# The first group's gather: token rows in two rounded parts, and one-pass products, in a hybrid decoder trunk

## The chip, the cores and the metric

The kernel runs on one core of a Trainium2 chip. The metric is the device time of one execution in microseconds. TensorE (PE) multiplies, VectorE (DVE), ScalarE (ACT) and GpSimd (POOL) do the elementwise work, and SyncE (SP) issues the large loads. 4-byte numbers come in two types here: fp32, whose product PE does in several passes, and fp32r, a rounded form whose product takes one pass.

## What is computed

Two layers work on 528 tokens of 1024 numbers: 16 meta tokens and 512 of the input. Layer 0 is a short convolution with gates, layer 1 is latent attention; each is followed by a mixture of experts. Of 64 experts of 256 columns, in 8 groups, each token picks one group, and in it the two best experts:

```
g_logits = xf @ w_grp ;  grp = argmax(g_logits)          # 8 groups
e_logits = xf @ w_exp                                    # 8 per group
top_p, top_i = top_k(softmax(e_logits of that group), 2)
gate   = p_g * top_p / sum(top_p)
expert = grp * 8 + top_i
out    = sum over both: gate * (silu(xn @ w_gate[e]) * (xn @ w_up[e])) @ w_down[e]
h      = h + out
```

## The kernel before

**Tiles.** The tokens lie in h as four tiles of 128 rows (0 to 3) and one of 16 (META, the tile hm). Layer 0 works on all five, layer 1 on the four.

**Weights.** A mixture of experts reads 192 MB per layer. `Ring` loads them in pieces of 1 MB over SP's queue into slots: four called A, up to 13 called R, and B, five in layer 0 and eight in layer 1. A slot takes the next piece of a fixed list as soon as its last reader is through. The B slots are opened at the start of `run`, in the order `LEFT[layer]`, in memory that the stage before used. SP's queue works in order: a load whose slot is not free holds up those behind it.

**The experts** run in 16 quads of four. gate_up (L589, gu) is the first product of each.

**The stretch around the change.** `project_out` (L266 to L298) does the last projection of a layer by three fp32r products of each pair of parts (L292) and adds it to h (L294). As soon as a tile of h is whole, `route` follows. It squares the rows (L231, ACT), transposes (L372), copies (L375 on ACT, L377 on DVE), multiplies for the logits (L380) and does the choice as a chain of small DVE instructions: gm, oh, mg, oh, se (L395), s (L397), eq, gt, eq, gt (L398 to L401), r and M (L402, L403). M says which experts a token has. `rank` (L411 to L425) counts tokens by a product with a triangle (L417) and makes from it rm (L418), d (L419) and aux (L421). d is the 0/1 matrix that picks the tokens of the first group.

`first_gather` (L457 to L477) collects the group's tokens. Each tile gives a small product pa (L467) and two products of 512 columns, d times h, in fp32 (L431, `gather_tile`), all accumulated in three banks. Behind the last tile come ag (L473, DVE), xg (L436, two instructions of ACT), sel (L441), the select (L450) and xT (L451), and then gate_up of quad 0. The later groups go through the same `gather_tile` from `run`. What stands where in an engine's row is decided by a scheduler from the order of the code and the data; `rank` of the last tile is put behind the third last tile's gather by hand.

Of the kernel before, what the change touches and what calls it, by code (L numbers as in the profile page):

```python
# [9 lines left out]
F32 = mybir.dt.float32  # L10
F32R = mybir.dt.float32r
BF16 = mybir.dt.bfloat16
I32 = mybir.dt.int32
AF = mybir.ActivationFunctionType
ALU = mybir.AluOpType
AX = mybir.AxisListType.X
ET = mybir.EngineType
PSUM = bass.MemoryType.PSUM

P = 128  # L20
D = 1024
# [9 lines left out]
SLOT = 2048  # L31
# [5 lines left out]
STEPS = ((0,), (1,), (2,), (3,), (4,), (5,), (6, 7)), ((4,), (5,), (6, 7))  # L37
NX = 3, 0
TOP = 13, 3
LEFT = range(5), (0, 1, 2, 4, 3, 5, 6, 7)  # L40
LAST = (0, 512), (512, D)
LATE = 12, 13

# [15 lines left out]
def rows(t):  # L59
    return NM if t == META else P  # L60
# [56 lines left out]
def trunk_kernel(ctx: ExitStack, tc: tile.TileContext, x, meta, const, masks, rope, gcol, grow, wr, w_in, w_out, w_a, w_qr, w_hp,  # L117
                 w_o, w_gate, w_up, w_down, out):
    nc = tc.nc
    V, A, T, G = nc.vector, nc.scalar, nc.tensor, nc.gpsimd  # L120
# [7 lines left out]
    h = [cp.tile([P, D], F32, name=f"h{t}") for t in range(4)] + [hm.tile([P, D], F32, name="hm")]  # L128
# [6 lines left out]
    for l in range(2):  # L135
        for a in range(4):
            c = G_FFN + 8 * l + 2 * a
# [114 lines left out]
    def pool(stack, name, bufs=1, side=None, space=None):  # L252
        kw = {} if space is None else {"space": space}
        return stack.enter_context(tc.tile_pool(name=name, bufs=bufs, side=side, reuse_waits="tile", **kw))
# [44 lines left out]
    class Moe:  # L299
# [124 lines left out]
                if s not in self.done:  # L424
                    T.matmul(self.rkv[:, s], one_b[:n], M[:n, t], start=False, stop=False, skip_group_check=True)  # L425

        def gather_tile(self, ps, t, first, last):

            n, d = rows(t), self.d[:rows(t), t].bitcast(F32)
            for u in range(2):  # L430
                i = T.matmul(ps[u], d, h[t][:n, 512 * u:512 * u + 512], start=first, stop=last, skip_group_check=True)  # L431
            return i

        def scaled_tokens(self, ps, ag):
            for u in range(2):
                A.activation(self.xg[:, :, 64 * u:64 * u + 64], ps[u].rearrange("s (p k) -> s k p", k=8), AF.Copy, scale=ag[:, 9:10])  # L436
# [17 lines left out]
        def new_ag(self):  # L454
            return self.ep.tile([P, 18], F32, tag="ag", name="ag", bufs=2)

        def first_gather(self, psum):  # L457

            def bank():
                return psum.tile([P, 512], F32, tag="acc", name="acc", bufs=5)  # L460

            self.sel = {}
            ps, pa = [bank(), bank()], bank()
            for t in self.done:
                first, last = t == self.done[0], t == self.done[-1]
                n = rows(t)
                T.matmul(pa[:, :10], self.d[:n, t].bitcast(F32), self.aux[:n, t, :10], start=first, stop=last)  # L467
                i = self.gather_tile(ps, t, first, last)
                if t == self.done[-3]:
                    with tc.issue_after(i.ins):  # L470
                        self.rank(self.done[-1])
            self.ag0 = self.new_ag()
            V.tensor_copy(self.ag0[:, :10], pa[:, :10])  # L473
            self.scaled_tokens(ps, self.ag0)
            self.choose(0, self.ag0)
            self.select(0, self.x0, bank)
# [63 lines left out]
        def run(self, limit, late, order, done=None, after=None, redo=None, again=None):  # L540

            layer, nT, tiles = self.layer, self.nT, self.tiles
            with ExitStack() as st:
                B = [(pool(st, f"ringB{layer}{i}"), f"B{i}") for i in range(NB[layer])]
                ring.open([B[i] for i in LEFT[layer]], limit)
                for a in ("gup", "psm", "ygp") if layer == 0 else ("psm", "gup", "ygp"):
# [323 lines left out]


    moe0 = Moe(0)
    with ExitStack() as l0:
        zp = pool(l0, "zp")
        zH = zp.tile([P, 8, NTOK], F32R, name="zH")
# [8 lines left out]
        with ExitStack() as l0a:  # L884
            wp = pool(l0a, "wp0", 2)
            psum = pool(l0a, "ps0", space=PSUM)
# [9 lines left out]
            def in_weights(j, s):  # L896
                raw = ring.get(("in", j, s))
                H, L = (wp.tile([P, SLOT], F32R, tag=a, name=a, bufs=2).rearrange("p (a c) -> p a c", a=8)
                        for a in ("wH", "wL"))
                for k in range(8):  # L900
                    i, _ = split_scaled(H[:, k], L[:, k], raw[:, k], gc[:, G_MIX0 + k:G_MIX0 + k + 1])
                ring.release(("in", j, s))
                loaded[j, s] = H, L
                return i
# [15 lines left out]
            first = in_weights(0, 0)  # L920
# [8 lines left out]
            for j in range(4):  # L929
                W = []  # L930
                for s in range(3):
# [3 lines left out]
                    for m in range(2):  # L935
                        mc = 2 * j + m
                        ps = psum.tile([P, 2, 512], F32, tag="acc", name="acc", bufs=3)
                        for k in range(8):
                            for l, r in ((wH, xH), (wH, xL), (wL, xH)):
                                for u in range(2):  # L940
                                    T.matmul(ps[:, u, :HALF], l[:, k, P * m:P * m + P], r[:, k, HALF * u:HALF * u + HALF],  # L941
                                             start=k == 0 and l is wH and r is xH, stop=k == 7 and l is wL)
                        pv = ps[:, :, :HALF]
                        if s == 0:
                            c = tp.tile([P, 2, HALF], F32, tag="c", name="c", bufs=2)
# [17 lines left out]
                            G.tensor_copy(zM[:, mc, :NM], acc[:, :NM])  # L963
        moe0.prepare(first_late)
        wp = pool(l0, "wp0b", 2)
        psum = pool(l0, "ps0b", space=PSUM)
        project_out(lambda j: [wp.tile([P, 512], F32R, tag=a, name=a) for a in ("wH", "wL")], psum, "out", zH, zL, zM, STEPS[0],
                    lambda t: moe0.route(t, psum))
        moe0.first_gather(psum)


    l1 = ExitStack()
# [27 lines left out]
    moe1 = Moe(1)  # L1000
# [4 lines left out]
    def weights(n):  # L1005
        return [wp.tile([P, SLOT], F32R, tag=a, name=a, bufs=2)[:, :n] for a in ("wH", "wL")]

    with l1:
# [18 lines left out]
        with side["wa_stack"] as la:  # L1027
            tp = pool(la, "tp1", 2, side="right")
            psum = pool(la, "ps1", space=PSUM)
# [120 lines left out]
        psum = pool(l1, "psa", space=PSUM)  # L1150
# [174 lines left out]
    psum = pool(psum_stack, "pso", space=PSUM)  # L1325
# [5 lines left out]
        return [w[:, 512 * (j - 4):512 * (j - 3)] for w in whole]  # L1331

    project_out(part, psum, "o", *oT[1], None, STEPS[1], lambda t: moe1.route(t, psum))
    moe1.first_gather(psum)
    psum_stack.close()
    oproj.close()

# [128 lines left out]
```

## Time and profile before

| | |
|---|---|
| three runs | 1394.77, 1397.29, 1398.41 us; median 1397.29 us |
| the profiled execution | 1394.88 us, its span 1393.1 us |
| mean granted clock of TensorE | 0.957 of full speed |
| busy: PE, DVE, ACT, POOL | 1245.3, 508.0, 313.4, 53.6 us |
| moved by DMA | 438.13 MB, mean 315 GB/s |
| chain that ended last | DMA 26%, PE 20%, ACT 1%, DVE 1% |
| L431 in `run` (later groups) | 224 records, 99.7 us, 598 ns of one |

PE is busy for 89% of the span, but that is a mean over stages with different limits. In the slices of the page the DMA moves some 420 GB/s in the two expert stages and less elsewhere. A product of fp32 shows as two records, so a product of 512 columns is a pair. Times below are in us from the start of the span.

### The profile page before, as it was taken

The numbers are of one execution on the slowest core, as the hardware profiler recorded it, in microseconds if no ns is written. First come the engines' busy times: TensorE is split into PE (matmuls) and PEld (weight loads), VectorE is DVE, ScalarE is ACT, GpSimd is POOL, SyncE is SP. The second block draws the span as 40 slices with busy tenths as digits, with TensorE's granted clock in tenths as the row PEclk, the third lists the DMA queues.
The fourth block names the chain that finished last, engine by engine and source line by source line (L and its number), as shares of the span: only waits on it lengthen the run. The fifth ranks groups of instructions, "written<-read, shape, count | busy, mean of one in ns | idle before, by whom it ended". The sixth has DMA issues, their size and how long they took to land. (4 is left out here: it accounts for less than half of the span.)

```text
span 1393.1 us, 22912 instructions
## 1 busy us (share of the span) xinstructions
PE 1245.3 (89%) x9647; PEld 795.4 (57%) x9647; DVE 508.0 (36%) x1220; ACT 313.4 (22%) x712; POOL 53.6 (4%) x146
## 2 busy tenths in 40 slices
PE   7999999999888798979779999999998797888885
PEld 7999866545444344434378888875543343434442
DVE  5555336132231312324336676562330212123124
ACT  6333123011010010121044775331111010101103
POOL 2100101000000000000021000010000000000001
PEclk9999999999999999989989999999999999999998
DMA  7422563899999999999810012959999999999995
GB/s 284 152 91 91 202 257 155 351 419 420 420 419 419 420 420 419 420 420 421 348 42 28 31 67 81 368 221 377 420 420 420 421 420 419 420 420 420 421 419 200
DMA packets 65957, 438.13 MB, mean 315 GB/s; under 512 B 7458, under 2 KB 7842, under 8 KB 15283
## 3 DMA queue, kind: packets, MB, share of 16 engines
q1 hardware_dynamic: 64432, 434.74, 76.4%
q10 hardware_dynamic: 1154, 1.78, 0.4%
q8 instruction: 81, 1.33, 0.4%
q14 instruction: 34, 0.27, 0.1%
q0 software_dynamic: 256, 0.01, 0.0%
HBM read 434.40 MB, written 2.10 MB: 313 GB/s over the span
## 5 line engine op out<-in xcount | busy, mean ns | idle before, releaser
L589 PE MATMUL gu<-R,xT 128*32 128x256 f32 x1856 | 162.1, 409 | 35.1 <-DMA R<-in_w_up_dram 24.6
L589 PE MATMUL gu<-B,xT 128*32 128x256 f32 x1376 | 144.4, 433 | 34.8 <-DMA B<-in_w_gate_dram 20.0
L589 PEld LDWEIGHTS gu<-R,xT 128*32 128x32 f32 x1856 | 78.0, 117 | 107.2 <-DMA R<-in_w_up_dram 33.7
L589 PEld LDWEIGHTS gu<-B,xT 128*32 128x32 f32 x1376 | 65.2, 124 | 94.3 <-issue 30.5
L589 PE MATMUL gu<-A,xT 128*32 128x256 f32 x720 | 100.5, 416 | 20.2 <-DMA A<-in_w_up_dram 13.3
L431 PE MATMUL w<-h,d 128*128 128x512 f32 x224 | 99.7, 598 | 0.0
L562 DVE COPY ag<-w 128x18 f32<-128x18 f32 x14 | 2.5, 177 | 240.5 <-PE w L561 240.5
L596 ACT ACTIVATE sg<-gu 128x256 f32<-128x256 f32 x32 | 12.3, 385 | 330.2 <-PE gu L589 330.2
L631 ACT ACTIVATE y<-dn 128x512 f32<-128x512 f32 x60 | 35.8, 597 | 199.7 <-PE dn L621 192.5
L941 PE MATMUL acc<-xH,wH 128*128 128x264 f32 x384 | 79.7, 288 | 0.0
L941 PE MATMUL acc<-xL,wH 128*128 128x264 f32 x384 | 78.9, 287 | 0.0
L941 PE MATMUL acc<-xH,wL 128*128 128x264 f32 x384 | 77.6, 283 | 0.0
L589 PEld LDWEIGHTS gu<-A,xT 128*32 128x32 f32 x720 | 45.1, 119 | 55.5 <-DMA A<-in_w_up_dram 17.9
L657 PE MATMUL w<-yHL,d 128*128 128x512 f32 (+1 forms) x252 | 73.0, 422 | 0.3
L659 DVE TENSOR_TENSOR h<-h,w 128x512 f32<-128x512 f32 x112 | 69.5, 679 | 0.8 <-PE w L657 0.5
L450 PE MATMUL w<-sel,xg 128*128 128x128 f32 x480 | 65.1, 293 | 4.5 <-ACT xg L436 4.5
L431 PEld LDWEIGHTS w<-h,d 128*128 128x128 f32 x224 | 41.4, 190 | 47.1 <-issue 46.4
L215 ACT ACTIVATE wH<-A,gc 128x256 fp32r<-128x256 f32 (+1 forms) x119 | 52.7, 520 | 59.0 <-PE acc L941 35.5
L450 PEld LDWEIGHTS w<-sel,xg 128*128 128x128 f32 x480 | 60.9, 206 | 7.2 <-ACT xg L436 7.2
L621 PE MATMUL dn<-R,sg 128*32 128x512 f32 x472 | 64.7, 604 | 0.0
L941 PEld LDWEIGHTS acc<-xL,wH 128*128 128x128 f32 x384 | 60.2, 189 | 0.0
L941 PEld LDWEIGHTS acc<-xH,wH 128*128 128x128 f32 x384 | 60.0, 190 | 0.0
(379 smaller groups left out, 2075.7 us busy)
## 6 DMA issues: line engine op xcount, KB each, us to landing
R<-in_w_up_dram SPq DMA_DIRECT2D x58, 1024.0 KB, 19.9
R<-in_w_down_dram SPq DMA_DIRECT2D x58, 1024.0 KB, 19.9
R<-in_w_gate_dram SPq DMA_DIRECT2D x58, 1024.0 KB, 19.9
B<-in_w_gate_dram SPq DMA_DIRECT2D x44, 1024.0 KB, 19.9
B<-in_w_up_dram SPq DMA_DIRECT2D x42, 1024.0 KB, 19.8
B<-in_w_down_dram SPq DMA_DIRECT2D x32, 1024.0 KB, 19.9
A<-in_w_down_dram SPq DMA_DIRECT2D x27, 1024.0 KB, 19.9
A<-in_w_gate_dram SPq DMA_DIRECT2D x26, 1024.0 KB, 19.9
```

The source lines that it names most:

```text
L215: i = A.activation(H, src, AF.Copy, scale=g)
L431: i = T.matmul(ps[u], d, h[t][:n, 512 * u:512 * u + 512], start=first, stop=last, skip_group_check=True)
L450: T.matmul(ps[:, k], self.xg[:, 4 * u + k], self.sel[q], start=True, stop=True)
L562: V.tensor_copy(ag, pa[:, :18])
L589: T.matmul(gu[CAP * e:CAP * e + CAP, s], xT[k // 4][:, k % 4, CAP * e:CAP * e + CAP], w[e][:, k], start=k == 0, stop=k == 7)
L596: A.activation(sg, gu[:, 0], AF.Silu)
L621: T.matmul(dn[CAP * e:CAP * e + CAP, :n], hT[:, b, CAP * e:CAP * e + CAP], w[:, b, c:c + n], start=b == 0, stop=b == 1)
L631: A.activation(y[:, u], down_part(q, hT, u, 0, 512 * u, 512), AF.Copy)
L657: T.matmul(ps[:m, :n], DT[t], a, start=i == 0, stop=i == 1)
L659: V.tensor_tensor(hh, hh, ps[:m, :n], op=ALU.add)
L941: T.matmul(ps[:, u, :HALF], l[:, k, P * m:P * m + P], r[:, k, HALF * u:HALF * u + HALF], start=k == 0 and l is wH and r is xH, stop=k == 7 ...
```

## The change

`split_rows` parts a tile of h into hH, the row rounded to fp32r by a copy on ACT, and hL, the rounded rest h - hH. It does so in two halves of 512 columns: DVE subtracts the first half, POOL the second. `gather_tile` then makes for each half two products in fp32r, d with hH and d with hL, in the place of one fp32 product. d is 0 or 1 and was stored in fp32r before. `first_gather` splits one tile ahead: tile j + 1 is split ahead of tile j's products. The later groups are gathered as before.

The parts need memory. In layer 0 it is a new pool `hs`, two tiles' worth, opened when the pools of the mixer have been closed; in layer 1 `room` cuts it from the two buffers that held the last projection's weights (so there the parts are called wH and wL). Both lie where B slots come later, and `LEFT` opens those slots last. From `gather_tile` on, lines of the changed kernel have numbers that are 14 to 17 higher.

```diff
-LEFT = range(5), (0, 1, 2, 4, 3, 5, 6, 7)
+LEFT = (2, 3, 4, 0, 1), (0, 1, 6, 7, 2, 4, 3, 5)
...
-        def gather_tile(self, ps, t, first, last):
-
-            n, d = rows(t), self.d[:rows(t), t].bitcast(F32)
+        def gather_tile(self, ps, t, first, last, parts=None):
+
+            n, d = rows(t), self.d[:rows(t), t]
             for u in range(2):
-                i = T.matmul(ps[u], d, h[t][:n, 512 * u:512 * u + 512], start=first, stop=last, skip_group_check=True)
+                c = slice(512 * u, 512 * u + 512)
+                if parts is None:
+                    i = T.matmul(ps[u], d.bitcast(F32), h[t][:n, c], start=first, stop=last, skip_group_check=True)
+                else:
+                    for j, a in enumerate(parts):
+                        i = T.matmul(ps[u], d, a[:n, c], start=first and j == 0, stop=last and j == 1, skip_group_check=True)
             return i
+
+        def split_rows(self, t, H, L):
+
+            n = rows(t)
+            for u, e in enumerate((V, G)):
+                c = slice(512 * u, 512 * u + 512)
+                A.activation(H[:n, c], h[t][:n, c], AF.Copy)
+                e.tensor_tensor(L[:n, c], h[t][:n, c], H[:n, c].bitcast(F32), op=ALU.subtract)
+            return H, L
...
-        def first_gather(self, psum):
+        def first_gather(self, psum, room):
...
-            for t in self.done:
+            parts = [self.split_rows(self.done[0], *room(0))]
+            for j, t in enumerate(self.done):
+                if j + 1 < self.nT:
+                    parts.append(self.split_rows(self.done[j + 1], *room(j + 1)))
...
-                i = self.gather_tile(ps, t, first, last)
+                i = self.gather_tile(ps, t, first, last, parts[j])
...
-        moe0.first_gather(psum)
+    with ExitStack() as l0, psum0:
+        hs = pool(l0, "hs", 2)
+        moe0.first_gather(psum, lambda i: [hs.tile([P, D], F32R, tag=a, name=a) for a in ("hH", "hL")])
...
-    moe1.first_gather(psum)
+    two_tiles = []
+
+    def room(i):
+        if i % 2 == 0:
+            two_tiles[:] = weights(SLOT)
+        return [w[:, D * (i % 2):D * (i % 2) + D] for w in two_tiles]
+
+    moe1.first_gather(psum, room)
```

How the rows of two engines change, in layer 0 at the last two tiles. PE's row before, from tile 2's gather to the last tile's; rk is the rank's bank, acc the gather's banks, and the number behind a name tells instances apart:

```order
L431 MATMUL acc_2471<-h2_65,d_122 128x512
L431 MATMUL acc_2472<-h2_65,d_122 128x512
L417 LDWEIGHTS tri_b_84
L417 MATMUL rk_2232<-M_1891,tri_b_84 128x72
L422 LDWEIGHTS one_b_87
L422 MATMUL rk_2232<-M_1891,one_b_87 128x64
L431 MATMUL acc_2471<-h3_66,d_122 128x512
L467 MATMUL acc_2473<-aux_117,d_122 128x10
L431 MATMUL acc_2472<-h3_66,d_122 128x512
```

PE's row now, in the same place and from tile 2's last two products:

```order
L436 MATMUL acc_2478<-hH_2508,d_122 128x512
L436 MATMUL acc_2478<-hL_2509,d_122 128x512
L417 LDWEIGHTS tri_b_84
L417 MATMUL rk_2232<-M_1891,tri_b_84 128x72
L422 LDWEIGHTS one_b_87
L422 MATMUL rk_2232<-M_1891,one_b_87 128x64
L436 MATMUL acc_2477<-hH_2525,d_122 128x512
L484 MATMUL acc_2479<-aux_117,d_122 128x10
L436 MATMUL acc_2477<-hL_2526,d_122 128x512
L436 MATMUL acc_2478<-hH_2525,d_122 128x512
L436 MATMUL acc_2478<-hL_2526,d_122 128x512
```

The last tile has four products behind d instead of two, and the last of each tile reads what POOL has written. DVE's row before, in the last tile's choice from s to M:

```order
L397 TENSOR_REDUCE s8_1894<-se_2459 128x8
L398 TENSOR_TENSOR eq_2461<-s8_1894 128x64
L399 TENSOR_TENSOR gt_2460<-s8_1894 128x64
L400 TENSOR_TENSOR eq_2461<-eq_2461,cs_58 128x64
L401 TENSOR_TENSOR gt_2460<-gt_2460,eq_2461 128x64
L402 TENSOR_REDUCE r8_1895<-gt_2460 128x8
L403 SCALAR_TENSOR_TENSOR M_1891<-r8_1895,oh_114 128x64
```

DVE's row now, in the same place and from the se ahead of s:

```order
L395 TENSOR_TENSOR se_2459<-misc_2444,oh_114 128x64
L419 TENSOR_SCALAR d_122<-cs_58,rm0_118 128x128
L421 TENSOR_REDUCE aux_117<-rm0_118 128x8
L397 TENSOR_REDUCE s8_1894<-se_2459 128x8
L445 TENSOR_TENSOR hL_2526<-h3_66,hH_2525 128x512
L398 TENSOR_TENSOR eq_2461<-s8_1894 128x64
L399 TENSOR_TENSOR gt_2460<-s8_1894 128x64
```

The last tile's subtraction has come between s and eq, and tile 2's d and aux, which stood ahead of the whole choice, are now in it. In layer 1 all of DVE's four subtractions stand ahead of the last tile's gm.

## Rows read from the trace of the kernel before

**Rows 1.** Windows in both layers: busy us of each engine, clock, DMA share, GB/s.

```profile
core 0: us, PE busy (x) PEld busy (x) DVE busy (x) ACT busy (x) POOL busy (x), PEclk, DMA share, GB/s
225.00:235.00 10.00, 10.00 (x49) 7.62 (x49) 4.06 (x19) 0.76 (x3) 0.00 (x0) 0.70 0.75 318
235.00:240.00 5.00, 4.54 (x19) 2.22 (x19) 4.32 (x26) 0.47 (x3) 0.00 (x0) 1.00 0.01 2
...
250.00:690.00 440.00, 388.68 (x3193) 191.58 (x3183) 120.68 (x250) 54.22 (x108) 0.00 (x0) 0.95 1.01 417
...
915.00:925.00 10.00, 10.00 (x73) 8.48 (x72) 7.53 (x32) 3.79 (x10) 2.61 (x9) 1.00 0.40 151
925.00:930.00 5.00, 5.00 (x31) 3.58 (x30) 3.75 (x17) 0.72 (x3) 0.00 (x0) 1.00 1.01 428
...
935.00:940.00 5.00, 3.44 (x45) 2.69 (x48) 2.44 (x10) 2.08 (x4) 0.00 (x0) 1.00 0.01 2
...
945.00:1360.00 415.00, 356.36 (x3001) 176.23 (x2993) 96.46 (x203) 45.26 (x90) 0.00 (x0) 0.95 1.01 420
```

**Rows 2.** The chain that ended last: start, length, what; a piece of many.

```profile
993.64 19.82 DMA R<-in_w_gate_dram
```

**Rows 3.** Timeline of SP's queue: start, length, what; the first loads behind each gather.

```profile
247.86 0.80 SPq L101 DMA_DIRECT2D R<-in_w_down_dram  x2
...
942.33 1.11 SPq L101 DMA_DIRECT2D A<-in_w_down_dram  x2
```

**Rows 4.** The chain in layer 1, ahead of quad 0: start, length, what.

```profile
919.99 0.96 PE acc L431 x2
...
921.41 0.86 PE acc L431 x2
...
927.26 0.96 PE acc L431 x2
...
932.83 1.12 PE acc L431 x2
...
934.08 0.97 PE acc L431 x2
935.08 0.70 ACT xg L436
...
938.65 7.24 PE gu L589 x128
```

**Rows 5.** Timelines of DVE and PE in layer 0, the last tile.

```profile
238.09 0.23 DVE L403 SCALAR_TENSOR_TENSOR M<-r,oh 128x64 bf16<-128x64 f32 x1
...
239.22 1.12 PE L431 MATMUL acc<-h,d 128*128 128x512 f32 x2
...
240.32 1.10 PE L431 MATMUL acc<-h,d 128*128 128x512 f32 x2
...
244.19 1.07 PE L589 MATMUL gu<-R,xT 128*32 128x256 f32 x16
```

**Rows 6.** Timeline of PE: two fp32r products of 512 columns in a row.

```profile
903.01 0.39 PE L292 MATMUL acc<-wH,oL 128*128 128x512 f32 x1
903.23 0.39 PE L292 MATMUL acc<-wH,oH 128*128 128x512 f32 x1
```

**Rows 7.** Lines with like shapes: ns min/median/max, first and last start, forms.

```profile
L375 ACT ACTIVATE hT<-tp x9: 218/597/598, 205.2 to 924.8; 128x512 f32<-128x512 f32 x8, 128x64 f32<-128x64 f32 x1
...
L212 DVE TENSOR_TENSOR yHL<-yg,yHL x32: 678/690/692, 292.6 to 1360.3; 128x512 fp32r<-128x512 f32 x32
...
L957 POOL TENSOR_TENSOR cv<-cv,r x8: 1322/1332/1502, 38.8 to 149.9; 128x528 f32<-128x528 f32 x8
...
L348 POOL TENSOR_TENSOR wg<-wg,gc x2: 1154/1196/1237, 188.2 to 894.8; 128x576 f32<-128x576 f32 x2
```

**Rows 8.** DVE's line L216 as a whole, and POOL's timeline at 45 us.

```profile
L216 DVE SCALAR_TENSOR_TENSOR wL<-A,gc,wH x119: 466/477/1554, 13.2 to 830.7; 128x256 fp32r<-128x256 f32 x108, 128x512 fp32r<-128x512 f32 x11
...
45.41 1.50 POOL L957 TENSOR_TENSOR cv<-cv,r 128x528 f32<-128x528 f32 x1 [5.22 <-DVE cv L955]
```

**Rows 9.** A window in layer 0 with a lower clock; columns as in rows 1.

```profile
225.00:231.00 6.00, 6.00 (x26) 4.78 (x26) 1.72 (x9) 0.00 (x0) 0.00 (x0) 0.50 1.00 423
```

More of the change, by code (lines that the diff above doesn't have):

```diff
@@ L872, in trunk_kernel @@
     moe0 = Moe(0)
+    psum0 = ExitStack()
     with ExitStack() as l0:
@@ L965, in trunk_kernel @@
         wp = pool(l0, "wp0b", 2)
-        psum = pool(l0, "ps0b", space=PSUM)
+        psum = pool(psum0, "ps0b", space=PSUM)
         project_out(lambda j: [wp.tile([P, 512], F32R, tag=a, name=a) for a in ("wH", "wL")], psum, "out", zH, zL, zM, STEPS[0],
                     lambda t: moe0.route(t, psum))
-        moe0.first_gather(psum)
+    with ExitStack() as l0, psum0:
+        hs = pool(l0, "hs", 2)
+        moe0.first_gather(psum, lambda i: [hs.tile([P, D], F32R, tag=a, name=a) for a in ("hH", "hL")])
     l1 = ExitStack()
```

## The prediction

> **What bounds the kernel now.** I read the windows first. From 250 to 690 us and from 945 to 1360 us, the expert stages of the two layers, the DMA engines are full: share 1.01 at 417 and 420 GB/s [rows 1]. The chain that ended last says the same: from 993.64 us on it is made of loads of some 19.8 us [rows 2]. So a faster engine in there brings nothing. Just ahead of each stage the DMA stands still: 2 GB/s in 235 to 240 us and again in 935 to 940 us [rows 1]. SP's queue shows why: its next loads are issued at 247.86 and 942.33 us, when quad 0 has read its first weights and slots come free [rows 3]. Quad 0 starts with gate_up, in layer 1 at 938.65 us [rows 4]. The rest of the kernel is therefore a block that is moved by as much as gate_up of quad 0 starts earlier or later, once in each layer. **The end moves by the sum of the two shifts**, and both lie at the edited gather.
>
> What sets that start: in layer 1 the chain shows PE until 928 us, with the fp32 gather of tiles 0 and 1 in it, then DVE's routing of the last tile, then from 932.83 us that tile's gather, xg, select and xT [rows 4]. In layer 0 the end is alike: DVE's M at 238.09, the gather at 239.22 and 240.32 us, gate_up at 244.19 [rows 5].
>
> **The products.** A pair of records of 512 fp32 columns takes 0.86 us where nothing else stands beside it (921.41 us [rows 4]). One-pass fp32r products of 512 columns follow each other by 903.23 - 903.01 = 0.22 us; over the neighbours it is 0.227 [rows 6]. Two of them, one for each part, take 0.45 us, so each half of a tile saves 0.41 us. There are 10 such halves in layer 0 and 8 in layer 1: 18 x 0.41 = 7.4 us of PE. How much of it is on the path?
>
> Layer 1: four halves stand ahead of the last tile's logits on the chain (0.86 to 0.96 us each, the first two and the last in [rows 4]); 4 x 0.41 = 1.6 us, if PE goes on setting the pace. Tile 2's are covered by DVE's routing in both kernels. The last tile's two begin at 932.83 and 934.08 us, and xg's second half waits for the last of them until 935.08 us [rows 4]. Afterwards the bank of half 0 is whole about 0.75 us after 932.83 us, and the two xg of 0.70 us run one behind the other: they end 0.7 us earlier. Bound by xg, not by the products, the last tile thus gains 0.7 us in each layer.
>
> **The copies on ACT.** 18 copies of 512 columns at 0.597 us [rows 7], 4.8 us in layer 1. ACT is busy 3.79 of 10 and 0.72 of 5 us there [rows 1]. They stand ahead of the last tile's copy L375, and in 915 to 925 us there are 6 us free to take them. I cost them at nothing; without that cover a pair would cost 1.2 us.
>
> **The subtractions on DVE.** Nine of 0.69 us [rows 7], 0.60 from start to start. In layer 1 DVE is busy 7.53 of 10 us in 915 to 925 and 3.75 of 5 in 925 to 930 [rows 1]: 11.3 of 15, 3.7 us free. Four subtractions take 2.4 us of these, so 1.3 are left. In layer 0 that of the last tile stands between its s and eq, in the chain itself: +0.60 us, with nothing to hide it.
>
> **The subtractions on POOL.** The nearest rows are 1.33 us for 528 columns and 1.20 us for 576 [rows 7], so 512 columns are about 1.06 to 1.29 us; I take 1.2. POOL is nearly empty, so its own time is no bound. But the trace shows what a long POOL operation with two SBUF inputs does to DVE: while L957 ran from 45.41 us, 1.50 us long, one of DVE's L216 took 1.55 us where the median of that line is 0.48 [rows 8]. So DVE stood about as long as POOL ran. The routing's eq, gt and M and the subtractions have such inputs. Four times 1.2 = 4.8 us in each layer are at stake; the bounds are nothing (POOL runs while DVE waits for PE) and all of it. I take half, 2.4 us: DVE is free about a quarter of this stretch, and some of its instructions read PSUM.
>
> **The sum for layer 1.** DVE's need in 915 to 930 us becomes 11.3 + 2.4 + 2.4 = 16.1 us of 15. So DVE takes PE's place as the pace, the 1.6 us of PE are not delivered, and the last logits' routing ends 1.1 us later. With the last tile's -0.7 that is +0.4 us. Bounds: PE still the pace, -1.6 - 0.7 = -2.3; all stalls felt, 11.3 + 2.4 + 4.8 - 15 - 0.7 = +2.8.
>
> **The sum for layer 0.** DVE has time there (4.06 busy of 10 us in 225 to 235 [rows 1]), and PE sets the pace, part of it at a granted clock of 0.50, the lower of its two levels, from 225 to 231 us [rows 9]. Six halves ahead of the last logits would save 2.5 us. Against that, PE's row now has waits for ACT, DVE and POOL: the first tile's products stand ahead of the next tile's transposes and logits, and the pool has room for two tiles, so that tile 3's copies start only when tile 1's products have read theirs. A chain of copy, copy and POOL's subtraction (0.6 + 0.6 + 1.2 = 2.4 us) follows each release. I take 0.4 of the 2.5 us. Then DVE's subtraction +0.6, a stall of POOL's last one inside eq to M of 0.4 (bounds 0 and 1.2), and the last products -0.7: -0.1 us. Bounds: -2.5 + 0.6 - 0.7 = -2.6, and 0.6 + 1.2 - 0.7 = +1.1 with nothing saved by PE.
>
> **The slots.** LEFT now fills the slots under the new tiles last, behind the gather: two in layer 0, four in layer 1, two of them behind its last tile. In SP's row nothing stands behind them but the loads of 247.86 and 942.33 us [rows 3]. 2 MB at 420 GB/s take 5.0 us; from the end of the gather's products (some 241.4 and 935.1 us) to those issues there are 6.5 and 7.2 us, and the quad that reads the two is not the first. So I cost the later loads at nothing; if the cover were gone, the stage would still move by no more than the DMA time not yet done, 5 us at the worst.
>
> Sum: +0.4 - 0.1 = +0.3 us. The profiled execution took 1394.88 us, 1.78 more than its span and 2.41 under the median of the three runs, 1397.29. So 1395.2 by the profiled execution, **1397.6 us** by the median.
>
> **Rivals.**
> 1. PE stays the pace and the stalls are not felt, 0.20. For it: DVE's free quarter, and POOL can run while DVE waits for PE. Against it: the 1.55 us [rows 8], three such beside L957. Half of the two low bounds (-4.9) gives -2.4: 1394.9 us. Only with all of them is it faster by more than 0.3%, 4.2 us, about what a measurement of this kernel can tell from no change.
> 2. Slower: POOL's subtraction holds DVE for its whole length, every time, 0.15. For it: [rows 8] are nearly whole lengths, and that POOL was itself lengthened to 1.50 us when DVE was first. Then layer 1 costs +2.8 and layer 0 +1.1; it turns the sign once more than 2.1 of the 4.8 us are felt in layer 1, and it reaches 1401.2 us, with PE's waits for POOL 1401.8.
> The Trainium skill, SBUF — State Buffer, section on the two separate sides, calls the port pair that the two share an exclusive lock: whoever starts first keeps it for the whole instruction and the other is blocked. The 1.55 us agree; by that rule this rival would hold whenever DVE has work, 1401.2 us. It also says that ACT and PE never wait on anyone, and no run here shows that for the copies of h.
> 3. The clock, 0.12 for both signs. Without the stretch at 0.50 PE would do its 6 us in 3, and behind POOL's waits about half of it arrives: -1.5, 1396.1 us. A new stretch at the lower level under gate_up of layer 1, 7.24 us [rows 4], would add some 3.6: 1401.2 us. For the first: the 16-row products ahead of the stretch become shorter. Neither can be read off beforehand.
> 4. The change doesn't do what it says, 0.05: one-pass products with d as weights go at 0.43 instead of 0.22 us. The last tile's gain is gone: +1.4, 1399.0 us.
> 5. The loads come too late, 0.03: 1397.6 + up to 5 us.
>
> **How the numbers follow.** The forecast itself has 0.45, with 1396 to 1399.5 us. Rival 1 goes down to 1394.9 (all of it 1392.4), rival 2 up to 1401.8; the three runs of before alone lie 3.6 us apart, so that the median of after may be off by 1.5 us. The range 1394.0 to 1401.8 leaves out about 2 in 10. Faster by over 0.3% needs nearly all of rival 1: 0.06. Slower by over 0.3% (above 1401.5) is the upper half of rival 2, a clock stretch in layer 1 and a little of 5: 0.09. Within: 0.85.
>
> **What would show it.** In the profile after: products of the gather 0.227 us apart and the last tile's xg 0.7 us earlier behind its d; POOL's subtractions 1.06 to 1.29 us, and beside them eq, gt, M or hL of DVE of over 1 us; between eq and M of layer 0's last tile a subtraction of 0.69 us; gate_up of quad 0 within 1 us of 244.19 and 938.65 us; SP's next loads right behind, and the DMA as full as before. I would be wrong if gate_up starts 2 us or more away from these, or if the DMA stage is no longer just moved.

## The result: 0.6% slower, and the profile after

| | before | after |
|---|---|---|
| median | 1397.85 us (1394.77 to 1398.86) | 1406.15 us (1402.89 to 1409.21) |
| ratio | | 1.0061, 95% interval 1.0047 to 1.0075 |
| profiled execution, its span | 1394.88, 1393.1 us | 1408.76, 1406.6 us |
| mean granted clock in it | 0.957 | 0.945 |
| busy: PE, DVE, ACT, POOL | 1245.3, 508.0, 313.4, 53.6 us | 1251.4, 517.4, 322.9, 66.0 us |

The change costs 8.3 us. The forecast was 1397.6 us in a range up to 1401.8, with a chance of 0.09 for slower by over 0.3%. The time lies above the range. The profiled execution of after is one of its longer ones, 2.6 us over its median, and that of before lies 3.0 us under its own, so the 13.5 us between the two spans show where time goes better than how much.

The block from the first product of a layer's last projection (L292, with its weight load) to SP's next load behind gate_up grew from 89.7 to 94.1 us in layer 0, from 50.8 to 58.0 us in layer 1. These are the 4.4 and 7.2 us of the table further down. Another 2.3 us lie between the blocks, in the last quads of layer 0, and the rest of the span is as long as before to 0.3 us. Gate_up of quad 0 starts at 248.40 and 950.29 us, 4.2 and 11.6 us later than before: the sign of being wrong that the prediction had named. SP's queue shows the two restarts, against 247.86 and 942.33 us [rows 3] (start, length, what):

```profile
243.89 0.80 SPq L101 DMA_DIRECT2D B<-in_w_down_dram  x2
252.07 0.80 SPq L101 DMA_DIRECT2D R<-in_w_down_dram  x2
...
944.93 1.08 SPq L101 DMA_DIRECT2D B<-in_w_down_dram  x2
956.04 0.80 SPq L101 DMA_DIRECT2D A<-in_w_down_dram  x2
```

The loads of the B slots that now come last start 8.2 and 11.1 us ahead of the restarts, and 2 MB take 5 us: they are hidden. What is not as before is TensorE's clock. Windows of after, with the columns of [rows 1]:

```profile
225.00:235.00 10.00, 9.37 (x43) 8.59 (x43) 6.92 (x22) 2.14 (x5) 2.66 (x3) 0.50 0.26 109
235.00:240.00 5.00, 4.55 (x16) 3.05 (x15) 3.77 (x15) 1.31 (x4) 1.27 (x1) 0.50 0.01 2
240.00:245.00 5.00, 3.16 (x9) 1.72 (x8) 2.93 (x19) 1.40 (x3) 0.00 (x0) 0.50 0.04 5
...
925.00:930.00 5.00, 5.00 (x41) 4.53 (x41) 4.53 (x16) 3.88 (x9) 2.19 (x4) 1.00 0.55 187
930.00:935.00 5.00, 3.25 (x23) 2.70 (x22) 4.90 (x21) 0.98 (x3) 1.73 (x3) 0.90 0.57 236
935.00:940.00 5.00, 4.55 (x18) 3.81 (x18) 1.67 (x10) 0.22 (x2) 0.00 (x0) 0.50 0.48 161
940.00:945.00 5.00, 4.51 (x12) 2.61 (x12) 3.71 (x24) 0.87 (x3) 0.00 (x0) 0.50 0.62 259
945.00:950.00 5.00, 3.78 (x16) 3.49 (x16) 2.31 (x10) 2.28 (x4) 0.00 (x0) 0.50 0.81 295
```

In layer 0 the lower of the two levels (0.50, 1.2 GHz) held for 225 to 231 us before [rows 9]; now it begins at the same place and holds to 248 us. So in layer 0 the fall itself is not new; what is new is that the clock does not come back. In layer 1, which ran the whole gather at 1.00, it holds from 934 us to the end of the select and on into gate_up. The chain that ended last shows what that does (start, length, what; the lines of before first, then those of after):

```profile
926.25 0.85 PE misc L380 x8
...
935.82 2.07 PE acc L450 x16
```

```profile
928.32 1.33 DVE wL L445
...
930.64 1.70 DVE wL L445
932.34 0.14 DVE M L403
...
936.79 1.63 PE misc L380 x8
...
945.73 3.80 PE acc L464 x16
...
950.29 9.31 PE gu L606 x128
```

The eight logits products, 0.85 us at the full clock, take 1.63; the select takes 3.80 us where it took 2.07; gate_up 9.31 where it took 7.24 [rows 4]. These three alone are 4.6 of the 7.2 us of layer 1. The products of the gather themselves are 0.24 us apart at the full clock and 0.42 at the lower one, nearly the price of the fp32 pair that they replace:

```profile
927.48 0.40 PE L436 MATMUL acc<-wH,d 128*128 128x512 f32 x1
927.72 0.39 PE L436 MATMUL acc<-wL,d 128*128 128x512 f32 x1
...
935.31 0.63 PE L436 MATMUL acc<-wL,d 128*128 128x512 f32 x1
935.73 0.63 PE L436 MATMUL acc<-wH,d 128*128 128x512 f32 x1
```

The second thing in the chain is the two long subtractions on DVE. Their timeline beside POOL's, with PE's two waits:

```profile
928.23 1.41 DVE L445 TENSOR_TENSOR wL<-h,wH 128x512 fp32r<-128x512 f32 x1
...
930.56 1.78 DVE L445 TENSOR_TENSOR wL<-h,wH 128x512 fp32r<-128x512 f32 x1
932.27 0.21 DVE L403 SCALAR_TENSOR_TENSOR M<-r,oh 128x64 bf16<-128x64 f32 x1
```

```profile
927.83 1.27 POOL L445 TENSOR_TENSOR wL<-h,wH 128x512 fp32r<-128x512 f32 x1 [2.64 <-ACT gl L396]
...
930.53 1.27 POOL L445 TENSOR_TENSOR wL<-h,wH 128x512 fp32r<-128x512 f32 x1
```

```profile
931.13 0.51 PE L372 MATMUL tp<-cs,h 128*128 128x128 f32 x2 [0.75 <-ACT hT L375]
932.53 0.19 PE L417 MATMUL rk<-M,tri_b 128*128 128x72 bf16 x1 [0.90 <-DVE M L403]
```

DVE's subtraction of 0.69 us takes 1.78 when POOL's began 0.03 us before it. M stands behind it in DVE's row, and PE waits 0.90 us for M. The 0.75 us ahead of that are a cover that went: before, a pair of the gather stood between the two sets of transposes (L372), while ACT copied the first set:

```profile
924.75 0.91 PE acc L431 x2
```

The parts were not ready for that place (DVE's second subtraction ends at 932.34 us), so PE stood. Right behind these two waits, in 930 to 935 us, the clock falls.

### The profile page after: what moved, and what is told of

It reads as the page before. It is cut to its first block, busy times and chain, and to the rows that moved or that the text cites. A ratio compares the mean times of both kernels' runs of the same rounds, so it can differ in the third digit from the quotient of the medians.

```text
span 1406.6 us, 22966 instructions
## 1 busy us (share of the span) xinstructions
PE 1251.4 (89%) x9647; PEld 803.3 (57%) x9647; DVE 517.4 (37%) x1229; ACT 322.9 (23%) x730; POOL 66.0 (5%) x155
## 3 DMA queue, kind: packets, MB, share of 16 engines
q10 hardware_dynamic: 1154, 1.78, 0.4%
## 5 line engine op out<-in xcount | busy, mean ns | idle before, releaser
L606 PEld LDWEIGHTS gu<-B,xT 128*32 128x32 f32 x1376 | 66.1, 124 | 94.5 <-issue 28.1
L959 PEld LDWEIGHTS acc<-xH,wL 128*128 128x128 f32 x384 | 59.7, 189 | 0.0
```

Of the source, the lines that this page charges most:

```text
L606: T.matmul(gu[CAP * e:CAP * e + CAP, s], xT[k // 4][:, k % 4, CAP * e:CAP * e + CAP], w[e][:, k], start=k == 0, stop=k == 7)
```

## The experiments

The theory from the two profiles: **lock** (POOL's subtraction holds DVE up, PE waits for DVE) and **clock** (a PE with fewer passes and more waits falls to the lower level, and everything to gate_up takes up to twice as long). In the expectations, **sparse** is the rival that the fewer passes alone let the clock fall. Other rivals: the order of the slots, the copies, the subtractions' own time.

The table gives each kernel's median beside the kernel before on the same chip. From one profiled execution of each come the two blocks defined above, and the time at the lower level in the 40 us ahead of the restart, from the granted clock of that window (before: 0.91 in layer 0, so 2 x 0.09 x 40 = 7.2 us). The last column is the granted clock over the whole span, as a mean over all executions that were timed, so it does not hang on the profiled one; but it counts the stretches under the full DMA as well.

| kernel | median, us | before, us | ratio (95%) | block 0, 1, us | lower level 0, 1, us | mean clock |
|---|---|---|---|---|---|---|
| before | 1397.85 | | | 89.7, 50.8 | 7.2, 0 | 0.957 |
| changed | 1406.15 | 1397.85 | 1.0061 (1.0047 to 1.0075) | 94.1, 58.0 | 24.0, 20.8 | 0.948 |
| e1_dve | 1400.17 | 1397.48 | 1.0027 (1.0012 to 1.0041) | 90.4, 53.8 | 13.6, 10.4 | 0.951 |
| e2_hH_only | 1394.46 | 1397.48 | 0.9972 (0.9959 to 0.9986) | 91.8, 53.0 | 24.0, 10.4 | 0.952 |
| e3_left | 1397.75 | 1397.48 | 0.9995 (0.9981 to 1.0008) | 89.6, 50.8 | 7.2, 0 | 0.957 |
| e4_split_fp32 | 1400.29 | 1397.48 | 1.0024 (1.0011 to 1.0037) | 90.9, 52.5 | 7.2, 0 | 0.958 |
| e5_twice | 1400.00 | 1397.67 | 1.0021 (1.0008 to 1.0034) | 94.5, 50.4 | 13.6, 0 | 0.958 |
| e6_last_dve | 1401.06 | 1397.67 | 1.0029 (1.0012 to 1.0046) | 89.1, 50.5 | 7.2, 0 | 0.952 |
| e8_dve_twice | 1398.39 | 1397.67 | 1.0008 (0.9994 to 1.0023) | 90.9, 49.6 | 3.2, 0 | 0.955 |
| e9_split_dve_fp32 | 1398.63 | 1397.67 | 1.0004 (0.9994 to 1.0014) | 91.6, 52.3 | 7.2, 0 | 0.958 |
| e10_last_left | 1397.44 | 1398.07 | 0.9997 (0.9985 to 1.0010) | 87.6, 50.5 | 3.2, 0 | 0.955 |
| e11_twice_l1 | 1404.32 | 1398.07 | 1.0037 (1.0017 to 1.0057) | 92.0, 50.4 | 13.6, 0 | 0.950 |
| e12_twice_l0 | 1402.38 | 1397.74 | 1.0047 (1.0028 to 1.0067) | 92.0, 56.5 | 7.2, 16.8 | 0.952 |
| e13_hH_twice | 1394.38 | 1397.74 | 0.9979 (0.9967 to 0.9991) | 88.7, 48.8 | 7.2, 0 | 0.955 |

How far the block and level columns may be read: where two kernels do the same work in a layer, they differ by up to 2.5 us in the block and up to 10.4 us in the time at the lower level (layer 0 of changed and of e11_twice_l1: 94.1 and 92.0, 24.0 and 13.6; layer 0 of e5_twice and of e12_twice_l0: 94.5 and 92.0, 13.6 and 7.2).

**The order of the slots alone (e3_left).** The kernel before, with

```diff
-LEFT = range(5), (0, 1, 2, 4, 3, 5, 6, 7)
+LEFT = (2, 3, 4, 0, 1), (0, 1, 6, 7, 2, 4, 3, 5)
```

> The kernel before with the changed order of the B slots alone. All theories: the same as the kernel before within 0.2%, 1396 to 1400 us. Rival slots: 2 us or more slower.

1397.75 against 1397.48 us: the order as such costs nothing.

**All subtractions on DVE (e1_dve).**

```diff
-            for u, e in enumerate((V, G)):
+            for u, e in enumerate((V, V)):
```

> All subtractions on DVE, none on POOL. Theory lock (POOL's subtraction holds DVE up, PE then waits for DVE, and with a PE that waits the granted clock falls to its lower level): no DVE instruction of the gather over 0.8 us, PE waits less at the last two tiles, and most of the 8.3 us come back: 1398 to 1401 us. Rival sparse (fewer and shorter PE passes alone let the clock fall, whoever subtracts): the half-clock stretches stay some 20 us long and the time stays at 1404 to 1407. Rival DVE work (nine subtractions of 0.69 us on a full DVE cost as much as the stalls): 1403 to 1406 with no long DVE instruction.

1400.17 us: 6.0 of the 8.3 us are gone. No subtraction is long any more (first the line of the kernel changed, then this one; ns min/median/max):

```profile
L445 DVE TENSOR_TENSOR wL<-h,wH x4: 684/1054/1782, 909.9 to 930.6; 128x512 fp32r<-128x512 f32 x4
```

```profile
L445 DVE TENSOR_TENSOR wL<-h,wH x8: 681/683/693, 904.4 to 929.6; 128x512 fp32r<-128x512 f32 x8
```

Eight subtractions of 0.68 us on DVE cost less than four with POOL beside them. The clock still falls, in layer 1 for 10.4 us and not 20.8 and so no longer under gate_up; the 13.6 us of layer 0 are within the spread, and the mean clock stays low, 0.951. PE still waits 0.94 us for M in layer 1, now behind DVE's own subtractions, where lock had expected less. So neither theory stands alone: without POOL there is less of the lower level, not none, and PE's wait is not POOL's alone.

**The parts made, but fp32 products (e4_split_fp32, e9_split_dve_fp32).** The gather ignores the parts:

```diff
-                i = self.gather_tile(ps, t, first, last, parts[j])
+                i = self.gather_tile(ps, t, first, last)
```

> The parts are made as in the changed kernel, but the gather multiplies h in fp32 as before; nobody reads the parts. Theory lock: DVE is held as in the changed kernel, and the last tile's gain is gone; 1402 to 1408 us. Rival sparse: PE has its fp32 work back, the clock stays up in layer 1 and the stretch in layer 0 is short; 1398 to 1400 us.

1400.29 us. The clock is that of the kernel before in both layers, with POOL's subtractions still there. But they hold DVE up less here, where other instructions stand beside them: no subtraction is long, and the lengthened instructions lose some 3 us over both layers, where those of the changed kernel lose some 5.7:

```profile
L445 DVE TENSOR_TENSOR wL<-h,wH x4: 674/684/693, 907.2 to 925.6; 128x512 fp32r<-128x512 f32 x4
```

So the parts and these smaller stalls cost 2.8 us as long as PE has its fp32 work; that the rest is all the sparse PE's does not follow from this run alone.

> The parts are made, all subtractions on DVE, and the gather multiplies in fp32; nobody reads the parts. Beside the same with POOL (1400.3 us) it tells stalls from DVE's own work. If the 2.8 us there are stalls: 1397 to 1398.5 us here. If they are the subtractions themselves: 1400 us or more here.

The same with (V, V): 1398.63 us, 1.0 over its kernel before. By the medians the other 1.8 us were POOL's; the intervals of the two ratios overlap by little (1.0011 to 1.0014).

**The second set of products (e5_twice, e8_dve_twice).** This gives PE its columns back and leaves the real products and the subtractions as they are. A function `again` repeats each one-pass product of a tile, behind the real ones, into a fourth bank that nobody reads:

```diff
+                self.again(idle, t, parts[j])
```

> The changed kernel, with every one-pass product of the gather made a second time into a bank that nobody reads, behind the tile's real ones: PE streams as many columns per tile as with fp32, about 1.8 us. POOL still subtracts half. Theory two causes (the stalls cost some 3 us, seen as 1400.3 us with fp32 products; the rest, some 6 us, is the half clock of a PE with too little to do): the half-clock stretches shrink to 7 us in layer 0 and none in layer 1, and the time falls to 1399 to 1402 us. Rival waits (the clock falls because PE waits for the parts, whatever it does between): 1404 to 1408 us, stretches of 20 us.

1400.00 us: 6.2 us less for work that is thrown away. In layer 1 the clock stays up, window by window:

```profile
930.00:935.00 5.00, 5.00 (x36) 4.38 (x37) 3.58 (x19) 0.35 (x2) 0.00 (x0) 1.00 0.00 0
935.00:940.00 5.00, 4.54 (x22) 3.10 (x21) 3.85 (x26) 1.42 (x4) 0.00 (x0) 1.00 0.95 356
```

PE is busy for all of 930 to 935 us, where the changed kernel had 3.25 of 5, although DVE's subtractions in layer 1 are as long as there (up to 1.69 us). So the lost time goes with the lower level. What lets the clock fall is not told by this run: the additional products also stand where PE waited, so that its wait for M is 0.57 us instead of 0.90 and that for ACT's copy is gone. The Trainium skill, TensorE: Matmul & The Clock Gate, in the section on the clock gate, says that the lower clock is the default state and that activity releases it; this run agrees, with 1.00 in these windows, where the changed kernel had 0.90 and 0.50.

> The same with all subtractions on DVE: no stall, and PE's work back. Theory two causes: both are gone, what is left is DVE's nine subtractions against the last tile's gain, 1396 to 1399 us. Rival waits: as with the subtractions on DVE alone, 1399 to 1402 us.

1398.39 us, a tie. With the kernels above this makes a square: without POOL's subtraction and with the second set 1398.4; with POOL's 1400.0; without the set 1400.2; with POOL's and without the set 1406.2. **Each cause alone costs 1.6 to 1.8 us, both together 7.8.** The single costs are not clear of noise: the intervals of the first three ratios overlap (0.9994 to 1.0023, 1.0008 to 1.0034, 1.0012 to 1.0041); that of the changed kernel (1.0047 to 1.0075) overlaps none of them. A reading that fits, but is not shown: at the full load PE rides over DVE's delays, at the thinned load the clock falls.

**Which layer (e11_twice_l1, e12_twice_l0).** The set in one layer alone, by a condition on the layer:

> The changed kernel with the second set of products in layer 1 alone. Theory: the layer-1 stretch at half clock is what the second set took away (the block from the projection to the restart was 58.0 us in the changed kernel, 50.4 with the set in both layers), and layer 0 gains nothing from it (94.1 against 94.5 us): 1399 to 1401 us, no half clock in layer 1, some 20 us of it in layer 0. Rival (both layers count alike): 1402 to 1404 us.

> The changed kernel with the second set of products in layer 0 alone; the set in layer 1 alone gave 1404.3 us, in both layers 1400.0 us. Theory both layers (the half clock costs about 4 us in layer 0 and 2 in layer 1): 1401 to 1403 us, half clock in layer 1 as in the changed kernel, less of it in layer 0. Rival (one stretch in layer 0 brings the other about, so the set in layer 0 is enough): 1399 to 1400.5 us, none in layer 1.

1404.32 and 1402.38 us: the set in layer 1 gives back 1.8 us, in layer 0 3.8, and in both 6.2. So by the medians both layers count, and my expectation of the first, read from the blocks of single profiled executions, was wrong. The shares are not settled: the intervals of both ratios overlap that of the changed kernel, and the ten executions of the first lie in two groups, three near 1397 us and seven from 1401 to 1407. In the second, layer 1 shows the lower level as the changed kernel does (16.8 us of 40).

**The rounded part alone (e2_hH_only, e13_hH_twice).** The rest hL is neither made nor multiplied, and so is left out of the gathered rows:

> No subtraction and no product with hL: the gather takes the rounded part alone, which leaves the rest of h out of the gathered rows. Copies on ACT, pools, order of the slots are those of the changed kernel. Theory lock: nothing holds DVE, gate_up of quad 0 starts earlier than in the kernel before by 1 to 3 us in each layer, 1393 to 1397 us. Rival sparse: PE has even less to do, the clock falls in both layers, 1403 us or more. Rival slots or copies (the loss lies in them): 1404 to 1407 us.

1394.46 us: faster by 0.28%, though the clock falls as far as in the changed kernel in layer 0. With only the copies left, the copies are no cause. The time is the one that lock expected, but not by its way: in the profiled execution gate_up starts at 246.39 and 938.54 us, no earlier than before (244.19 and 938.65), and both blocks are longer than before, by 2.1 and 2.2 us. That execution took 1397.05 us, 2.6 over the median, so the trace does not show where the gain comes from, and why the lower level costs so little here is not settled.

> The gather takes the rounded part alone, without subtraction, so that the rest of h is left out of the gathered rows; and each of its products is made twice more into a bank that nobody reads, so that PE streams six one-pass products per tile. Without these additional products it was 1394.5 us, with half clock for 24 us in layer 0 and 10 in layer 1. Theory two causes: without stalls, and with the clock kept by work, 1390 to 1393 us, half clock under 10 us in layer 0 and none in layer 1. Rival (the clock falls because PE waits): as without them, 1394 to 1396 us.

1394.38 us, no gain over e2_hH_only by the median, though the profiled execution has the clock of the kernel before and blocks 3.1 and 4.2 us shorter than there. The theory expected 1390 to 1393, so here its rival held. The blocks hold what the additional products cost, so that cost does not explain it; but the two profiled executions lie 3.0 us under and 2.6 us over the medians of their kernels. Where no subtraction is made, these runs show no price of the lower level.

**Only the last tile in two parts (e6_last_dve, e10_last_left).** The tiles ahead in fp32, DVE alone subtracts:

```diff
-            parts = [self.split_rows(self.done[0], *room(0))]
+            two = self.split_rows(self.done[-1], *room(0))
...
-                i = self.gather_tile(ps, t, first, last, parts[j])
+                i = self.gather_tile(ps, t, first, last, two if last else None)
```

> Only the last tile of each layer in two parts and one-pass products, both halves subtracted on DVE; the tiles ahead in fp32 as in the kernel before. Theory two causes: no stall, PE's work ahead of the last tile as before and so the clock as before, xg of quad 0 0.7 us earlier behind d in each layer: 1395 to 1397 us, a tie or just faster than the kernel before. Rival: the few fp32 products less at the end are enough to let the clock fall under gate_up: 1399 us or more.

1401.06 us, though both blocks are shorter than before (89.1 and 50.5 us). The profiled execution loses most of its time behind the second restart: from there to the end it takes 455.6 us, where before took 450.8 and every other kernel of the table 450.6 to 453.4. That points to the slots. With one pair of parts in layer 1, all four late loads stood behind the last tile's gather, since SP's queue keeps its order. They ran on behind the restart at 943.29 us:

```profile
920.92 15.58 SPq L101 DMA_DIRECT2D B<-in_w_up_dram  x4
936.54 1.22 SPq L101 DMA_DIRECT2D B<-in_w_down_dram  x2
943.29 1.72 SPq L101 DMA_DIRECT2D A<-in_w_down_dram  x2
```

```profile
935.00:940.00 5.00, 3.33 (x28) 2.56 (x32) 4.17 (x24) 2.87 (x5) 0.00 (x0) 1.00 0.65 229
940.00:945.00 5.00, 5.00 (x100) 3.01 (x92) 0.12 (x1) 0.00 (x0) 0.00 (x0) 1.00 1.01 418
```

The DMA was full across the restart, where that of the kernel before stood at 2 GB/s just ahead of it [rows 1]: the stage began with a backlog.

```diff
-LEFT = (2, 3, 4, 0, 1), (0, 1, 6, 7, 2, 4, 3, 5)
+LEFT = (1, 2, 3, 4, 0), (0, 1, 6, 7, 3, 5, 2, 4)
```

> As the kernel with only the last tile in two parts, but its parts lie under one B slot in layer 0 and two in layer 1, and LEFT opens just these last. There, four loads of layer 1 stood behind the last tile's gather, 4 MB or about 9.8 us at 420 GB/s, against 6.7 us from their issue at 936.54 to the next load at 943.29. Theory late loads (the 3.4 us of that kernel are these loads running on behind the restart): 2 MB fit in now, DMA is idle again just ahead of the restart, 1395 to 1398 us, level with the kernel before or just under it. Rival clock (the loss there is a lower clock in the expert stages): still 1400 us or more.

With only the slots under the parts opened last: 1397.44 us, 3.6 less, and the late loads start 7.6 us ahead of the restart:

```profile
932.07 0.80 SPq L101 DMA_DIRECT2D B<-in_w_down_dram  x2
939.67 0.80 SPq L101 DMA_DIRECT2D A<-in_w_down_dram  x2
```

That is level with the kernel before (0.9997, 0.9985 to 1.0010). The mean clock rose as well, from 0.952 to 0.955, so this run does not wholly part the late loads from a lower clock in the expert stages. No version with both parts beat it.

## Why the prediction was wrong

- **Where the time is decided: right.** The expert stages only moved, but for 2.3 us ahead of layer 1 in the profiled execution. There the clock is 0.66 in 675 to 685 us, against 1.00 in the same work before:

```profile
675.00:685.00 10.00, 5.36 (x48) 2.21 (x50) 2.04 (x4) 1.15 (x2) 0.00 (x0) 0.66 1.02 386
```

  In the profiled executions of the other kernels such short falls lie elsewhere in this stage, so I count that to the spread of 6 us among the runs of after.
- **The products: right in price, wrong in what they bring.** 0.227 us was 0.24 where the clock was up. The 0.7 us of the last tile came about in e6_last_dve and e10_last_left: from its first product to the select it is 2.31 us in both layers of both, where it was 2.99 before. In the changed kernel, where that tile runs at the lower level, it is 3.28.
- **The copies on ACT: at nothing, right** (e2_hH_only).
- **The subtractions on DVE: right in order.** e9_split_dve_fp32 puts all of it, without POOL, at 1.0 us, which is not clear of no change (0.9994 to 1.0014); the sum had 0.6 for it, in layer 0.
- **The subtractions on POOL: too short by little, the stalls right.** Taken at 1.2 us, bounds 1.06 to 1.29; measured 1.26 to 1.40. The stalls cost 1.6 to 1.8 us in both layers together as long as PE has its work; the sum had charged layer 1 with 1.1 us for DVE and layer 0 with 0.4.
- **The slots: right for the changed kernel, by e3_left and the restarts.** Rival 5 is real, though: e6_last_dve beside e10_last_left puts it at some 3 us.
- **The clock: the step that failed.** The sum took away 7.4 us of PE's work and added waits on three engines ahead of PE, and left the clock as it was: a term put at nothing. In its place the runs showed 24.0 and 20.8 us at the lower level ahead of the two restarts, against 7.2 and 0, and 6.2 of the 8.3 us given back once PE had its columns again (e5_twice). Rival 3 had seen a new stretch, but gave the clock 0.12 for both signs together, put the stretch under gate_up of layer 1 alone, at 3.6 us, and said that it couldn't be read off. In layer 1 it began in the last tile's logits; in layer 0 it began where it had before and did not end at 231 us. Row 9 was the warning: layer 0 fell even with the fp32 work.
- **The rivals were priced one by one.** Rival 2 (stalls) was right that DVE is held, though not every time (POOL's subtraction at 922.68 us lengthened none), and by itself that is worth under 2 us; on top of the thinner products it is worth 6.0 (e1_dve beside the changed kernel). A chance for both at once was not in the cases.

What stays open: which of the thinner work and the waits lets the clock fall first. The square shows that both are needed for the full loss. Nor is it shown why e2_hH_only, with long stretches at the lower level, is as fast as e13_hH_twice and faster than all others; where no subtraction is made, that pair shows no price of the lower level.

## What to carry to other kernels

Before taking passes away from TensorE ahead of a critical chain, ask what keeps its clock up there: cheaper products that leave the engine waiting can slow down the work behind them by more than they save. Don't lay two-input work on POOL beside a DVE chain; the whole of it on DVE was cheaper here. And where slots are lent out, open last only those that are lent, since a queue in order makes every load behind the first late one late too.

## What was not expected of the hardware

- Work that is thrown away made the kernel 6.2 us faster (1406.15 to 1400.00 us); the granted clock stayed at 1.00 in 930 to 945 us, where the changed kernel was at 0.50 from 935 us on.
- The clock fell in layer 1 while PE was still busy for 3.25 of 5 us, with no single wait above 0.90 us.
- DVE's subtraction of 0.69 us took up to 1.78 us beside POOL's of 1.27, and a small gt of 0.22 us up to 1.31:

```profile
225.06 1.31 DVE L399 TENSOR_TENSOR gt<-s 128x64 f32<-128x64 f32 x1
```
